# Two merge gates as seven-block products with features on the partitions, and a new layout of that phase's entry, borders and exit

## The chip, the cores and the metric

The kernel runs on one core of one Trainium2 chip. The metric is the device time of one execution in microseconds (us), the median of several runs. A profile is one execution recorded by the hardware profiler. PE is TensorE's matmul stream and PEld its weight loads, DVE is VectorE, ACT ScalarE, POOL GpSimd, and SP the engine that issues most transfers; L12 is line 12 of the kernel.

## The reference

One layer of a decoder trunk on 512 tokens of width 2048, all in float32. A normalised and modulated input `u` is projected once into the columns of three token mixers: A (differential attention), B (retention) and C (dilated windows). Each mixer's output is multiplied by a SiLU gate, projected back to width 2048, and the three are added under merge gates:

```python
u = rms_norm(x, norm_w) * (1.0 + scale[:, None]) + shift[:, None]
proj = jnp.einsum('bsd,de->bse', u, w_in)          # values, queries, keys, z, and g_a, g_b, g_c
...
y_a = jnp.einsum('bsw,wd->bsd', o_a.astype(dt) * jax.nn.silu(a_z), w_proj_a)   # y_b, y_c alike
merged = jax.nn.sigmoid(g_a) * y_a + jax.nn.sigmoid(g_b) * y_b + jax.nn.sigmoid(g_c) * y_c
y = jnp.einsum('bsd,de->bse', merged, w_out)
return x + gate[:, None] * y
```

`shift`, `scale` and `gate` (the adaLN modulation) are products of silu(c) with `w_ada`. A last RMSNorm follows.

## The kernel before, in words

**Arithmetic.** A float32 product is made of three matmuls: every operand is split into a high part that TensorE takes (`...h`, cast on ACT) and the rest (`...l`, a subtraction on DVE), and `mm3` (L144-148) adds h·h, l·h and h·l into one PSUM bank. `w_half` (L130) loads 1024 x 128 weights (`wr`, 512 KB on SP's queue) and splits them into `wh`, `wl`. `proj` (L150) multiplies 2048 x 128 weights with all 512 tokens: 2 x 8 blocks x 3 = 48 matmuls of 128x512, features on the partitions; between its halves it may call a function, `mid`. There are eight PSUM banks: two of the tag `pj` (projections), six of `at`.

**Stages.** By the trace of before, in us from the span's start: the modulation, `u` and sixteen blocks of C's merge gate (to 239); the seven-block phase (239 to 667); eight heads of C (671 to 1374); C's merge (to about 1470); heads of A (to 1765) and A's merge (to about 2045); heads of B (to 2249) and B's merge (to about 2515); the output product and the last norm.

**Seven-block phase** (L474-626). The five value matrices (2048 x 1024 each: three of C, one each of A and B) are multiplied by a scheme that splits tokens, depth and columns in two and needs seven block products where eight are usual. `unit_jobs` (L524) makes 14 jobs for one matrix of 1024 columns: P1, P2 and R3 take weights as they are (two jobs each), and eight jobs take sums of weights, one block row j each, for R6, R5, R7 and Q4. A job is 24 matmuls of 128x512; stationary are 128 tokens, moving are 512 columns. A job's preparation loads weights (`xr`, 1 MB), sums them if need be on DVE, casts `xh` on ACT and subtracts `xl` on DVE; it is issued one job ahead. The token side is fixed: four sums of token blocks, `fh` and `fl`, which `forms_build` (L496) makes from the stored `u` for two j at a time, ahead of each of the first four jobs. `keep`, `p2_done` and `sum_done` take results out of PSUM and store them to `v_dram` from GpSimd's queue (`store`).

**Entry.** The last seven raw products of C's gate are copied out of their banks by `spill` (L395), alternately on ACT and DVE, through two buffers `raw`, and stored to `graw_dram` from ACT's queue. The phase's first products, P1 of unit 0, go to `at` banks.

**Exit.** After the phase the weight pool `wp2` opens on the side where the forms lay. In the heads of C, `bias_step` (L723) works out columns of C's gate bias: four loads `bw` on SP, multiplications and sums on POOL (L641-647), and a product on TensorE (L652). It is called in heads 0, 2 and so on.

**Merges.** `gate_phase` (L656) walks over 16 blocks `db` of 128 output columns. C's ("first") loads the raw gate (`gsg`), takes the sigmoid, and stores gate times y to `part_dram`. A's ("mid") and B's ("last") compute the gate with `proj` (48 matmuls) in the block before its use, then y with 24 matmuls (`y_start`: six of the eight heads' rows; the last two after it), multiply (L700), add the part sum `gpr` (L702), which has one buffer, and store (A) or split (B) the result. In A's merge `gate_aux` also makes the adaLN gate: 32 parts, three a block, each a load `gwa` of 512 KB and two operations on DVE (L1042, L1044).

**The end of a mixer.** Head 7's last steps are put off (`left`) and run as the `mid` of the first gate projections. For A they are the turn of the softmax to keys on the partitions (transposes L943, casts L950), the values' products, and `rms_gate` (L902): a sum of squares (L896-900, L905), a root (L907), a reciprocal (L908), two multiplications, and the split of y (`yh`, L212; `yl`, L213). For B they are two heads' values and `rms_gate`s.

The order in each engine's queue is made by a scheduler from the order of the code and the buffers. SP issues its transfers in order; a transfer that waits for a buffer holds those behind it.

Of the kernel before, what the change touches and what calls it, by code (L numbers as in the profile page):

```python
# [64 lines left out]
def hybrid_kernel(ctx, tc, x, c, w_in, w_pa, w_pb, w_pc, w_out, w_ada, b_ada, norm_w, lam,  # L65
# [24 lines left out]
    graw_dram = dram.tile([KC, P, S], F32, tag="graw", name="graw")  # L90
    gate_dram = dram.tile([1, D], F32, tag="gated", name="gated")
# [313 lines left out]
    for i, (phase, k) in enumerate(steps):  # L405
# [34 lines left out]
        if k == KC - 1:  # L440
            for b in range(NF):
                spill(ps[b], b + phase * (NF + NM), b % 2 == 0)
# [53 lines left out]
    def forms_build(g):  # L496

        r = wxp.tile([P, 4, 512], F32, tag="xr", name="xr", bufs=3)
        for i in range(2):
            nc.sync.dma_start(out=r[:, 2 * i:2 * i + 2, :],  # L500
                              in_=u_dram[i * HJ + 2 * g:i * HJ + 2 * g + 2].rearrange("j p t -> p j t"))
        for jj in range(2):
            d = evp.tile([P, 4, 256], F32, tag=("z", "s")[jj], name="d")
            a11, a21 = r[:, jj, 0:256], r[:, jj, 256:512]
            a12, a22 = r[:, 2 + jj, 0:256], r[:, 2 + jj, 256:512]
            dve.tensor_sub(d[:, 0, :], a21, a22)
            dve.tensor_sub(d[:, 1, :], a11, d[:, 0, :])
            dve.tensor_sub(d[:, 3, :], a21, a11)
            dve.tensor_sub(d[:, 2, :], a12, d[:, 1, :])
            j = 2 * g + jj  # L510
            act.copy(fh[j], d)
            dve.tensor_sub(fl[j], d, fh[j].bitcast(F32))

    def stat(name, j, q):

        qs = slice(q * P, (q + 1) * P)
        if name in "0123":
            return fh[j][:, int(name), qs], fl[j][:, int(name), qs]
        k = j if name == "A11" else HJ + j
        if name == "A22":  # L520
            qs = slice(256 + q * P, 256 + (q + 1) * P)
        return uh[k][:, qs], ul[k][:, qs]

    def unit_jobs(w, c0, out):  # L524
# [10 lines left out]
        def pure_mul(key, name, t, hl):  # L535
            if t == 0:
                st[key] = [at() for _ in range(2)]
            for jj in range(4):
                j = 4 * t + jj
                for q in range(2):  # L540
                    mm3(st[key][q], *stat(name, j, q), hl[0][:, jj, :], hl[1][:, jj, :], j == 0, j == HJ - 1)
# [7 lines left out]
        def store(t, half, cc):  # L549
            nc.gpsimd.dma_start(out=out[half * 256:half * 256 + 256, cc:cc + 512].rearrange("(q p) c -> p q c", p=P),  # L550
                                in_=t)

        def p2_done():
# [3 lines left out]
            store(t, 0, 0)  # L557
# [13 lines left out]
        def sum_mul(j, hl):  # L571
# [4 lines left out]
            for key, name, s in (("R6", "1", 3), ("R5", "0", 0), ("R7", "3", 1), ("Q4", "A22", 2)):  # L576
                for q in range(2):
                    mm3(st[key][q], *stat(name, j, q), hl[0][:, s, :], hl[1][:, s, :], j == 0, j == HJ - 1)

        def sum_done():  # L580
# [8 lines left out]
            store(r3, 0, 512)  # L589
# [3 lines left out]
            store(s, 1, 512)  # L593
            for q in range(2):
                dve.tensor_sub(z[:, q, :], st["Q4"][q], z[:, q, :])
            store(z, 1, 0)

        jobs = []
        for key, name, k0, cc, done in (("P1", "A11", 0, 0, lambda: keep("P1", "p1")),
                                        ("P2", "A12", 1024, 0, p2_done),  # L600
                                        ("R3", "2", 1024, 512, lambda: keep("R3", "r3"))):
            for t in range(HJ // 4):
                jobs.append((lambda k0=k0, cc=cc, t=t: pure_prep(k0 + t * 512, c0 + cc),
                             lambda hl, key=key, name=name, t=t: pure_mul(key, name, t, hl),
                             done if t == HJ // 4 - 1 else None))
        for j in range(HJ):
            jobs.append((lambda j=j: sum_prep(j), lambda hl, j=j: sum_mul(j, hl),
                         sum_done if j == HJ - 1 else None))
        return jobs


    jobs = []
# [15 lines left out]
    wp_es, wp = open_pool("wp2", "right", reuse_waits="tile")  # L628
    y_es, yp = open_pool("yp", "right")
    g_es, gp = open_pool("gp", "right")  # L630
# [25 lines left out]
    def gate_phase(g0, w_p, mode, mh=None, ml=None, left=(), then=None, aux=None):  # L656
# [4 lines left out]
        def run_left():  # L661
            if left:
                left.pop(0)()

# [7 lines left out]
        def gate_cols(db):  # L672
# [5 lines left out]
            else:  # L678
                act.activation(out=sgs[db], in_=proj(g0 + db * P, mid=run_left), func=AF.Sigmoid)

        if mode == "first":
            for db in range(3):
                ahead[db] = y_start(db)
                run_left()
        gate_cols(0)
        for db in range(KC):
            if db + 1 < KC:
                gate_cols(db + 1)
            while left:
                run_left()  # L690
# [17 lines left out]
            if aux is not None:  # L708
                aux()


    c_es, cp = open_pool("cp", "left")
# [142 lines left out]
    for hd in range(8):  # L855
# [16 lines left out]
        if hd == 0:  # L872
# [15 lines left out]
    gate_phase(G_C, w_pc, "first", left=left)  # L888
    c_es.close()
# [112 lines left out]

    gm_es, gmp = None, None

# [251 lines left out]
```

## Time and profile before

| | |
|---|---|
| median of 3 runs | 2702.05 us (2701.15 to 2705.34) |
| the profiled execution | 2704.7 us, span 2702.9, mean granted clock 0.989 |
| TensorE busy | 2602.8 us, 96%, 11939 matmuls |
| DVE, ACT, POOL busy | 1531.2, 990.5, 231.5 us |
| moved by DMA | 405.01 MB, 150 GB/s over the span |

A row of a timeline has the start, the length, the engine and line, what is written from what, partitions x elements, a count, and in brackets the idle time ahead with what ended it. A matmul's recorded length overlaps the next one's, so the time a matmul takes from TensorE is the distance of two starts. A row of windows has, after the stretch and its length, each engine's busy us with a count in the order PE, PEld, DVE, ACT, POOL, then the granted clock (1.00 is full speed), the busy share of the DMA engines and GB/s. A row of waits has the waiting line, what it waited for, the us in total, the number of times and the longest. A row of groups has the count, then busy us and the mean ns of one, then the idle time ahead.

### The profile page before, as it was taken

The numbers are of one execution on the slowest core, as the hardware profiler recorded it, in microseconds if no ns is written. First come the engines' busy times: TensorE is split into PE (matmuls) and PEld (weight loads), VectorE is DVE, ScalarE is ACT, GpSimd is POOL, SyncE is SP. The second block draws the span as 40 slices with busy tenths as digits, with TensorE's granted clock in tenths as the row PEclk, the third lists the DMA queues.
The fourth block names the chain that finished last, engine by engine and source line by source line (L and its number), as shares of the span: only waits on it lengthen the run. The fifth ranks groups of instructions, "written<-read, shape, count | busy, mean of one in ns | idle before, by whom it ended". The sixth has DMA issues, their size and how long they took to land.

```text
span 2702.9 us, 30651 instructions
## 1 busy us (share of the span) xinstructions
PE 2602.8 (96%) x11939; PEld 2148.6 (79%) x11939; DVE 1531.2 (57%) x2283; ACT 990.5 (37%) x1399; POOL 231.5 (9%) x217
## 2 busy tenths in 40 slices
PE   7897999999999999999999999999999999999998
PEld 5675777777778888888888888888888777888888
DVE  7983877778333434444344677667336786333334
ACT  4222433333333333433333566642223454222222
POOL 3331000000231022220100000000000000000000
PEclk9998999999999999999999999999999999999999
DMA  9774666664543434434355222349544333333532
GB/s 348 246 272 159 229 210 213 217 205 166 148 113 98 133 106 110 133 98 133 102 171 164 85 79 86 94 145 307 148 143 119 86 94 96 115 114 101 206 102 102
DMA packets 467002, 405.01 MB, mean 150 GB/s; under 512 B 23509, under 2 KB 390823, under 8 KB 465703
## 3 DMA queue, kind: packets, MB, share of 16 engines
q1 hardware_dynamic: 442854, 371.49, 44.8%
q10 hardware_dynamic: 19714, 16.86, 1.8%
q0 software_dynamic: 4288, 14.72, 1.5%
q8 instruction: 93, 1.52, 0.2%
q14 instruction: 53, 0.43, 0.1%
HBM read 371.48 MB, written 31.53 MB: 149 GB/s over the span
## 4 chain that ended last, share of the span: by engine, by line
PE 78%; DVE 3%; issue 3%; DMA 2%; ACT 1%; POOL 1%; SPq 0%; DVEq 0%; POOLq 0%; ACTq 0%
PE pj L146 16%; PE pj L148 16%; PE pj L147 16%; PE at L148 9%; PE at L147 9%; PE at L146 9%; DMA bw<-in_w_in_dram 1%; DMA wr<-in_w_in_dram 1%; DVE rt L1073 1%; DVE wl L142 1%; DVE k1l L981 0%; PE at L925 0%; PE at L828 0%; PE at L781 0%; PE at L924 0%
## 5 line engine op out<-in xcount | busy, mean ns | idle before, releaser
L148 PE MATMUL pj<-uh,wl 128*128 128x512 f32 x2064 | 810.2, 393 | 13.0 <-DVE wl L142 10.5
L146 PE MATMUL pj<-uh,wh 128*128 128x512 f32 x2064 | 813.9, 394 | 3.6 <-ACT wh L141 3.6
L147 PE MATMUL pj<-ul,wh 128*128 128x512 f32 x2064 | 807.8, 391 | 0.0
L142 DVE TENSOR_TENSOR wl<-wr,wh 128x1024 fp32r<-128x1024 f32 x290 | 360.5, 1245 | 546.9 <-ACT wh L141 528.2
L141 ACT CAST wh<-wr 128x1024 fp32r<-128x1024 f32 x292 | 306.9, 1052 | 798.1 <-PE pj L147 588.3
L148 PEld LDWEIGHTS pj<-uh,wl 128*128 128x128 f32 x2064 | 390.0, 189 | 97.5 <-DVE wl L142 13.1
L146 PEld LDWEIGHTS pj<-uh,wh 128*128 128x128 f32 x2064 | 390.3, 189 | 82.9 <-ACT wh L141 4.2
L147 PEld LDWEIGHTS pj<-ul,wh 128*128 128x128 f32 x2064 | 390.4, 189 | 78.5
L146 PE MATMUL at<-yh,wh 128*128 128x512 f32 x384 | 149.7, 390 | 0.0
L148 PE MATMUL at<-yh,wl 128*128 128x512 f32 x384 | 149.6, 389 | 0.0
L147 PE MATMUL at<-yl,wh 128*128 128x512 f32 x384 | 149.5, 389 | 0.0
L567 ACT CAST xh<-xr 128x2048 fp32r<-128x2048 f32 x40 | 76.5, 1914 | 133.3 <-DVE xr L566 67.9
L146 PE MATMUL at<-xh,uh 128*128 128x512 f32 x240 | 95.5, 403 | 23.6 <-ACT xh L531 23.6
L566 DVE TENSOR_TENSOR xr<-xr 128x512 f32<-128x512 f32 x160 | 109.1, 689 | 8.8 <-DMA xr<-in_w_in_dram 5.6
L568 DVE TENSOR_TENSOR xl<-xr,xh 128x2048 fp32r<-128x2048 f32 x40 | 91.6, 2291 | 27.5 <-ACT xh L567 27.5
L700 DVE TENSOR_TENSOR gsg<-at,gsg 128x512 f32<-128x512 f32 x48 | 33.1, 690 | 117.1 <-PE at L148 93.8
L147 PE MATMUL at<-xl,uh 128*128 128x512 f32 x240 | 96.3, 401 | 2.9 <-DVE xl L532 2.9
L147 PE MATMUL at<-xl,fh 128*128 128x512 f32 x240 | 95.0, 396 | 1.4 <-DVE xl L532 1.4
L148 PE MATMUL at<-xh,ul 128*128 128x512 f32 x240 | 96.0, 400 | 0.0
L532 DVE TENSOR_TENSOR xl<-xr,xh 128x2048 fp32r<-128x2048 f32 x30 | 68.6, 2288 | 47.5 <-ACT xh L531 47.5
L148 PE MATMUL at<-xh,fl 128*128 128x512 f32 x240 | 94.8, 395 | 0.0
L146 PE MATMUL at<-xh,fh 128*128 128x512 f32 x240 | 94.0, 395 | 0.0
(365 smaller groups left out, 3835.7 us busy)
## 6 DMA issues: line engine op xcount, KB each, us to landing
wr<-in_w_in_dram SPq DMA_DIRECT2D x260, 512.0 KB, 3.9
xr<-in_w_in_dram SPq DMA_DIRECT2D x80, 512.0 KB, 4.0
xr<-in_w_in_dram SPq DMA_DIRECT2D x30, 1024.0 KB, 5.4
wa<-in_w_ada_dram SPq DMA_DIRECT2D x20, 1024.0 KB, 9.9
gwa<-in_w_ada_dram SPq DMA_DIRECT2D x32, 512.0 KB, 5.6
wr<-in_w_out_dram SPq DMA_DIRECT2D x32, 512.0 KB, 3.9
wr<-in_w_in_dram SPq DMA_DIRECT2D x32, 448.0 KB, 5.7
wb<-in_w_ada_dram SPq DMA_DIRECT2D x12, 1024.0 KB, 9.3
```

What stands on the lines that cost most here:

```text
L141: act.copy(h, r)
L142: low.tensor_sub(l, r, h.bitcast(F32))
L146: nc.tensor.matmul(ps, lhsT=ah, rhs=bh, start=start, stop=False)
L147: nc.tensor.matmul(ps, lhsT=ah, rhs=bl, start=False, stop=False)
L148: nc.tensor.matmul(ps, lhsT=al, rhs=bh, start=False, stop=stop)
L532: dve.tensor_sub(l, r, h.bitcast(F32))
L566: dve.tensor_add(r[:, o, :], r[:, o, :], r[:, a, :])
L567: act.copy(h, r)
L568: dve.tensor_sub(l, r, h.bitcast(F32))
L700: dve.tensor_mul(sg, py, sg)
L1073: dve.tensor_mul(t2[to:to + 32, :], ps[at_:at_ + 32, :], sin[at_:at_ + 32, :])
```

## The change

1. **The gates of A and B move into the seven-block phase.** Each gate (2048 columns) becomes two more units, so there are nine. They are computed feature-major (`fm`): stationary are 128 columns of weights, moving are 256 tokens, and a job is 48 matmuls of 128x256. `put_gates` takes the sigmoid and stores to `gate_of`. A's and B's merges load it and multiply y alone.
2. **Entry.** The first job's weights are prepared before the raw copies are queued, the copies go through four tiles that are two blocks wide each, and P1 goes to `pj` banks. The token sums are built for one j per job, over the first eight jobs, and the order of jobs is: P1 and P2 of unit 1, all of unit 0, then R3 and the sums of unit 1 (whose P1 goes through `p1_dram`), then the other units.
3. **Exit.** `wp2` opens on the left side and stays open to the end; the bias loads move from SP's queue to GpSimd's; the `bias_step` of head 0 moves to head 1.
4. **Merges.** All three start y for three blocks ahead, with one step of `left` after each. The adaLN gate is spread over C's merge and A's, 16 parts each, one a block (two in the first).

```diff
+    def block_mul(pss, name, j, h, l, fm):
+        if fm:
+            b = tokens(name, j, slice(0, 256))
+            for cb in range(4):
+                cs = slice(cb * P, (cb + 1) * P)
+                o = pss[cb // 2][:, (cb % 2) * 256:(cb % 2) * 256 + 256]
+                mm3(o, h[:, cs], l[:, cs], *b, j == 0 and cb % 2 == 0, j == HJ - 1 and cb % 2 == 1)
+        else:
+            for q in range(2):
+                mm3(pss[q], *tokens(name, j, slice(q * P, (q + 1) * P)), h, l, j == 0, j == HJ - 1)
...
+    def put_gates(g, b0):
+        def put(t, half, cc):
+            act.activation(out=t, in_=t, func=AF.Sigmoid)
+            b = b0 + cc // P
+            nc.gpsimd.dma_start(out=gate_of[g][b:b + 4, :, half * 256:half * 256 + 256].rearrange("b p t -> p b t"),
+                                in_=t.rearrange("p q (a t) -> p (q a) t", a=2))
+        return put
...
-    jobs = []
-    for unit, c0 in ((2, C_V), (3, C_V + 1024), (4, C_V + 2048), (0, A_V), (1, B_V)):
-        jobs += unit_jobs(w_in, c0, v_dram[unit])
+    units += [unit_jobs(w_in, g + b0 * P, put_gates(g, b0), fm=True) for g in (G_A, G_B) for b0 in (0, 8)]
+    jobs = units[1][0] + units[0][0] + units[0][1] + units[1][1]
+    for plain, summed in units[2:]:
+        jobs += plain + summed
     ready = jobs[0][0]()
+    for n, b in enumerate([NF - 1] + list(range(NF - 1))):
+        if n % 2 == 0:
+            t = evp.tile([P, 2, 512], F32, tag=("p1", "c", "r3", "s")[n // 2], name="raw")
+        (act.copy if n % 2 == 0 else dve.tensor_copy)(t[:, n % 2, :], ps[b])
+        nc.scalar.dma_start(out=graw_dram[NF + NM + b], in_=t[:, n % 2, :])
     for i, (_, mul, done) in enumerate(jobs):
-        if i < HJ // 2:
-            forms_build(i)
         nxt = jobs[i + 1][0]() if i + 1 < len(jobs) else None
+        if i < HJ:
+            form_build(i)
         mul(ready)
...
-            nc.sync.dma_start(out=r, in_=w_in[q * 512:(q + 1) * 512, G_C + db * P:G_C + (db + 1) * P]
+            nc.gpsimd.dma_start(out=r, in_=w_in[q * 512:(q + 1) * 512, G_C + db * P:G_C + (db + 1) * P]
...
-                act.activation(out=sgs[db], in_=proj(g0 + db * P, mid=run_left), func=AF.Sigmoid)
-        if mode == "first":
-            for db in range(3):
-                ahead[db] = y_start(db)
-                run_left()
+                nc.sync.dma_start(out=sgs[db], in_=gate_of[g0][db])
+        for db in range(3):
+            ahead[db] = y_start(db)
+            if left:
+                left.pop(0)()
...
+    def gate_aux(db):
+        for _ in range(2 if db == 0 else 1):
+            if gsum:
+                gate_sum()
+            if db < KC - 1:
+                gate_part()
...
-        if hd == 0:
+        if hd == 1:
             bias_step()
...
-    gate_phase(G_C, w_pc, "first", left=left)
-    c_es.close()
+    gate_phase(G_C, w_pc, "first", left=left, then=lambda: gate_open(c_es), aux=gate_aux)
+    gm_es.close()
```

What the change does to the order in ACT's queue is shown at three places. Lines of the changed kernel are a few further on: its L144 is L141 of before, its L549 L531, its L215 L212.

At the entry, ACT before: `raw` are the copies of raw gate products, `xh` the cast of a job's weights, `fh` the token sums.

```order
L398 COPY raw<-at 128x512
L401 DMA graw<-raw 128x512 x2
L398 COPY raw<-at 128x512
L401 DMA graw<-raw 128x512 x2
L398 COPY raw<-at 128x512
L401 DMA graw<-raw 128x512 x2
L398 COPY raw<-pj 128x512
L401 DMA graw<-raw 128x512
L531 CAST xh<-xr 128x2048
```

And now:

```order
L549 CAST xh<-xr 128x2048 x2
L650 COPY raw<-at 128x512 x2
L651 DMA graw<-raw 128x512
L650 COPY raw<-pj 128x512
L651 DMA graw<-raw 128x512 x5
L650 COPY raw<-at 128x512
L517 CAST fh_1820<-d 128x1024
L651 DMA graw<-raw 128x512
L549 CAST xh<-xr 128x2048
```

Two casts of weights now stand ahead of the copies, and no store stands between the first two copies.

At the exit of the phase, ACT now: `r`, `s` and `z` are results of the last gate unit, `wh` the first weights of C's head 0.

```order
L581 CAST xh<-xr 128x2048 x6
L633 ACTIVATE r_7294<-r_7294 128x1024
L633 ACTIVATE s<-s 128x1024
L633 ACTIVATE z<-z 128x1024
L144 CAST wh<-wr 128x1024 x5
```

Before, the casts of `wh` followed those of `xh` at once; three sigmoids now stand between them.

In A's tail, ACT before: `gsg` is a gate of the merge, `wh` the weights of gate projections and of y, the rest head 7's last steps.

```order
L141 CAST wh<-wr 128x1024
L896 ACTIVATE sq<-at 64x512
L896 ACTIVATE rs<-at 64x512
L899 CAST sqs<-sq 64x512
L141 CAST wh<-wr 128x1024
L679 ACTIVATE gsg<-pj 128x512
L907 ACT_TABLE_LOAD
L907 ACTIVATE rs<-at,eps 128x512
L212 CAST yh_4441<-rs 128x512
```

And now:

```order
L1034 CAST pth<-at 128x4x128
L980 ACTIVATE sq<-at 64x512
L980 ACTIVATE rs<-at 64x512
L983 CAST sqs<-sq 64x512
L991 ACT_TABLE_LOAD
L991 ACTIVATE rs<-at,eps 128x512
L215 CAST yh_7804<-rs 128x512
L144 CAST wh<-wr 128x1024 x3
```

No weights are cast and no gate is made between head 7's steps; the weights of y for the next blocks come behind its end.

More of the change, by code (lines that the diff above doesn't have):

```diff
@@ L439, in hybrid_kernel @@
             mod_step(2 if i == 0 else 1)
-        if k == KC - 1:
+        if k == KC - 1 and phase == 0:
             for b in range(NF):
-                spill(ps[b], b + phase * (NF + NM), b % 2 == 0)
+                spill(ps[b], b, b % 2 == 0)
             if phase == 0:
@@ L556, in p2_done @@
                 dve.tensor_add(t[:, q, :], st["p1"][:, q, :], st["P2"][q])
-            store(t, 0, 0)
+            put(t, 0, 0)
+            if early:
+                nc.gpsimd.dma_start(out=p1_dram, in_=st["p1"])
         def sum_prep(j):
```

196 lines of the change are left out of this document (93 added, 103 removed).

## The prediction

> **What bounds the kernel now.** I read the page first, then PE's waits, then PE's timeline at each wait.
>
> ```profile
> PE 2602.8 (96%) x11939; PEld 2148.6 (79%) x11939; DVE 1531.2 (57%) x2283; ACT 990.5 (37%) x1399; POOL 231.5 (9%) x217
> PE 78%; DVE 3%; issue 3%; DMA 2%; ACT 1%; POOL 1%; SPq 0%; DVEq 0%; POOLq 0%; ACTq 0%
> PE at L146 <- ACT xh L531: 23.6, 5, 17.5
> PE at L652 <- POOL br L647: 6.7, 1, 6.7
> PE at L781 <- DVE kc L188: 4.3, 1, 4.3
> ```
>
> TensorE is busy 96% of the span and owns 78% of the chain. Time is won by fewer or shorter matmul slots, or at the few waits; the largest, 17.5 us, stands where the seven-block phase begins. The terms below are made against the profiled execution (2704.7 us, span 2702.9); the median of the runs shown, 2702.05, lies 2.7 lower. A measurement of this kernel can tell about 0.2%, 5.4 us, from no change.
>
> **1. Gate products.** Starts of matmuls: the first of a gate's 48 and the first after them; then two 256-wide ones of the output product, 14 steps apart; then a weight load.
>
> ```profile
> 1812.30 0.39 PE L146 MATMUL pj<-uh,wh 128*128 128x512 f32 x1
> ...
> 1823.18 0.39 PE L146 MATMUL at<-yh,wh 128*128 128x512 f32 x1
> 2679.27 0.28 PE L146 MATMUL pj<-lh,mh 128*128 128x256 f32 x1
> ...
> 2680.92 0.28 PE L148 MATMUL pj<-lh,ml 128*128 128x256 f32 x1
> L148 PEld LDWEIGHTS pj<-uh,wl 128*128 128x128 f32 x2064 | 390.0, 189 | 97.5 <-DVE wl L142 13.1
> ```
>
> A 512-wide slot is 10.88/48 = 0.2267 us, a 256-wide one 1.65/14 = 0.1179. Two gates leave 2 x 16 x 48 = 1536 wide slots (348.2 us); four units bring 4 x 14 x 48 = 2688 narrow ones (316.9): **-31.3**. Bounds: 0.1200, the longest step between those rows, gives -25.6; half a wide slot, 0.1133, gives -43.6. I take the middle row, because it too changes its 128x128 weights at each matmul.
>
> The Trainium skill (TensorE: Matmul & The Clock Gate, "The mechanism") says that a weight load overlaps running matmuls only when its row group differs, and "LDWEIGHTS" there prices a load at 128/1.2 = 107 ns. By that rule a narrow slot would be 107 + 107 ns, an estimate of 0.213 us, and the phase would cost 575 us. The 0.1179 of the row disagrees: loads of 189 ns are recorded and the next start still comes after 118.
>
> **2. Entry.** TensorE's last raw product, the phase's first matmul, the second unit's and the third's first (one job of 24 into each unit); windows; ACT's last raw copy; what VectorE does from 238.8 to 300, by groups.
>
> ```profile
> 238.67 0.39 PE L434 MATMUL pj<-uh,wl 128*128 128x512 f32 x1
> 256.57 1.22 PE L146 MATMUL at<-xh,uh 128*128 128x512 f32 x2 [17.51 <-ACT xh L531]
> 351.75 0.63 PE L146 MATMUL at<-xh,uh 128*128 128x512 f32 x2
> 353.90 0.50 PE L146 MATMUL at<-xh,uh 128*128 128x512 f32 x1 [1.52 <-ACT xh L531]
> 431.93 0.64 PE L146 MATMUL at<-xh,uh 128*128 128x512 f32 x2
> 256.00:262.00 6.00, 4.33 (x9) 3.01 (x10) 4.94 (x9) 1.97 (x3) 0.00 (x0) 0.50 0.33 95
> 268.00:274.00 6.00, 5.32 (x24) 4.00 (x23) 3.72 (x5) 4.71 (x5) 0.00 (x0) 1.00 0.94 343
> 253.63 0.58 ACT L398 COPY raw<-pj 128x512 f32<-128x512 f32 x1 [7.34 <-DMA graw<-raw]
> L532 DVE TENSOR_TENSOR xl<-xr,xh 128x2048 fp32r<-128x2048 f32 x6 | 13.7, 2288 | 10.3 <-ACT xh L531 10.3
> L512 DVE TENSOR_TENSOR fl<-d,fh 128x1024 fp32r<-128x1024 f32 x8 | 9.4, 1218 | 0.5 <-ACT fh L511 0.5
> L509 DVE TENSOR_TENSOR d<-xr,d 128x256 f32<-128x256 f32 x8 | 3.3, 417 | 0.0
> ```
>
> A steady unit, border included, takes 431.93 - 351.75 = 80.2; less the border (1.7, its 1.52 of wait and the hop) 78.5, so 0.2336 per matmul and 5.6 per job. From 238.67 to 351.75 lie 113.1, for one unit and one job, 84.1: the entry loses 29.0 (the wait, half clock 0.50 behind it, and some waits on VectorE). The cause is ACT: its raw copies wait for their own stores with two buffers, up to 7.34, and the first xh cast stands behind them. Now the cast is ahead, the copies have four tiles, and P1 uses banks that the raw products leave free. What can be late next: in the first eight jobs (44.8 of TensorE) VectorE has eight xl (18.3), eight fl (9.7), 32 subtractions (13.3), and some 4 us of copies and sums, 45 to 46; the loads are 8 MB of weights, 4 of tokens and 2 to 3 of raw stores, near 45 us at the 343 GB/s row. Both are as long as the cover, so I leave 5 us: **-24** (2 to 12 left: -27 to -17).
>
> **3. Exit, and head 0 and 1 of C.** The last sums on VectorE, the first weight cast, TensorE behind it, and the clock after each of the three waits.
>
> ```profile
> 668.53 1.28 DVE L595 TENSOR_TENSOR z<-at,z 128x512 f32<-128x512 f32 x2
> 669.59 1.04 ACT L141 CAST wh<-wr 128x1024 fp32r<-128x1024 f32 x1 [11.75 <-DMA wr<-in_w_in_dram]
> 670.69 0.50 PE L146 MATMUL pj<-uh,wh 128*128 128x512 f32 x1 [3.63 <-ACT wh L141]
> 671.00:677.00 6.00, 5.52 (x19) 4.09 (x18) 2.74 (x3) 2.10 (x2) 0.00 (x0) 0.72 1.07 353
> 729.00:735.00 6.00, 6.00 (x23) 4.99 (x23) 2.68 (x7) 2.70 (x3) 0.00 (x0) 0.72 0.56 175
> 768.00:774.00 6.00, 6.00 (x16) 4.74 (x17) 0.76 (x2) 0.00 (x0) 2.23 (x3) 0.53 0.48 134
> ```
>
> Before: waits 3.6, 4.3 and 6.7 and, in 6 us each at a clock of 0.72, 0.72 and 0.53, 1.7, 1.7 and 2.8 us of lost speed: 20.8. After: the weight tiles are free early, but the order puts three sigmoids ahead of the first cast on ACT. The last can start only when the sums end, at 669.81; with one cast's 1.04 as its price it ends near 670.9, and the weight cast at 671.9. So the first wait grows by 1.3, to 4.9. POOL's bias sum is as near to its use as before, only a head later: its 6.7 and 2.8 stay. The wait on kc had its loads behind bias loads on SP's queue, which move to GpSimd's; I leave 1. (Behind the bias loads on GpSimd's queue stand only POOL's own sums and the small transfers of the head.) Sum 4.9 + 1.7 + 9.5 + 1 = 17.1: **-4** (-10, if the bias sum comes free too, to +2).
>
> **4. Borders.** Four borders of 1.7 become eight. A gate unit's hoisted matmul is half as wide; between nothing and 1.7 I take 0.9 for each of the four: **+3** (0 to +7).
>
> **5. Tails of A and B.** Gate projections covered head 7's tails; now 18 products of y, 4.1 us, stand at each place. The last score, the last softmax block, the squares, and the root of norms:
>
> ```profile
> 1759.93 0.40 PE L925 MATMUL at<-k1l,q 128*128 128x512 f32 x1
> 1773.20 0.75 DVE L934 SCALAR_TENSOR_TENSOR e<-e,st 128x512 f32<-128x512 f32 x1
> 1784.54 0.59 ACT L896 ACTIVATE sq<-at 64x512 f32<-64x512 f32 x1 [0.99 <-PE at L148]
> 1787.14 0.69 DVE L900 TENSOR_TENSOR sqs<-sq,sqs 64x512 fp32r<-64x512 f32 x1 [0.69 <-ACT sqs L899]
> 1791.57 1.28 ACT L907 ACT_TABLE_LOAD   x1
> 1793.59 3.35 DVE L908 RECIPROCAL rs<-rs 128x512 f32<-128x512 f32 x1 [1.40 <-ACT rs L907]
> 1798.49 0.62 ACT L212 CAST yh<-rs 128x512 fp32r<-128x512 f32 x1 [4.93 <-DVE rs L910]
> ```
>
> A: scores end at 1760.3; 21 projections (4.8) and 18 y reach 1769.2, the last block is ready at 1773.95; three y and ten transposes fill about 1.2: 3.5 of wait. The values' squares take 1784.54 to 1787.83, 3.3, under 18 y: no wait. From the norm's product to yh lie 7.5 with the table load (1791.57 to 1799.11), 6.2 without; six y cover 1.4: 4.8 to 6.1, taken 5.6. A: 9.1. B, from the end of its last projection: 18 y, values, 18 y, norm, values, 18 y end at 16.5. Head 6's chain (6.1 of products, 3.3 of squares, PE free at 10.2, then 7.5) gives yh at about 17.9: 1.4 of wait. One rs tile serves both heads, so head 7's squares follow yl: 1.3 more; then its 6.2, uncovered, 6.1. B: 8.8. The two last waits are longer than the 4.3 above and earn its 1.7 of slow clock each: **+21** (12 to 28).
>
> **6. Merges.** Stage rows of A's merge, and the part sum's addition and its loads (the answer on its tile):
>
> ```profile
> 1840.00:1860.00 20.00, 20.00 (x90) 16.58 (x89) 14.31 (x20) 5.23 (x6) 0.00 (x0) 1.00 0.96 303
> 1860.00:1880.00 20.00, 20.00 (x90) 16.55 (x89) 15.26 (x20) 5.42 (x7) 0.00 (x0) 1.00 0.99 332
> L702 DVE TENSOR_TENSOR gsg<-gsg,gpr x32: 672/692/693, 1801.4 to 2519.6; 128x512 f32<-128x512 f32 x32
> DMA to landing us min/median/max: 2.6/3.6/6.4
> ```
>
> A block of y is 24 x 0.2267 = 5.44 us. In A's merge it moves 512 KB of weights, 512 of the adaLN gate, 256 of gate, 256 of part sum in and 256 out: 1.835 MB, which at the mean of those rows, 317 GB/s (share 0.96 and 0.99, so no more is to be had), takes 5.79. Fifteen blocks: +5, and some at its uneven start: +9 (3; 25 if the single part-sum buffer sets the round at 6.4 + 0.7 = 7.1). C's merge moves 1.57 MB, 5.0, under 5.44: +2 (0 to 8). B's has no adaLN part: 0. **+11**. In the phase each gate unit adds four sigmoids to ACT, 1.04 each by the cast's row. What is queued behind one is the next xh cast; one job lies between that cast and its use, 5.6 us, so they are hidden while ACT keeps under it: **+1** for where two meet.
>
> **Sum:** -31.3 - 24 - 4 + 3 + 21 + 11 + 1 = -23.3: 2681.4 for such an execution, 2679 against the median.
>
> **Rivals.**
> (a) The loads of A's merge set its pace at the part sum's 7.1 us, and C's at 6.0. For: shares of 0.96 to 0.99 already with a third of the products now taken away. Against: the median landing is 3.6, a round of 4.3. It adds 16 + 6: 2701. By the Trainium skill (DMA: Bandwidth & Descriptors, "Anatomy of one DMA", for GpSimd's path) 256 KB take 2.0 + 0.6 us, an estimate of 2.6; the trace's minimum agrees, its median and maximum do not.
> (b) Slower: y's weights come one block late. SP issues in order, and a part-sum load waits for the last block's sum with the next weights behind it. If only one block lies between, a block takes the addition 0.7, a landing of 5.0 (between 3.6 and 6.4), cast 1.04, subtraction 1.2: 7.9, so 2.5 x 13 blocks in A and as much in B, +65 less the 9 of A: 2735. It decides from 6.6 us a block on. Against: the order issues weights three blocks ahead.
> (c) The entry is bound by VectorE or DMA: 20 us stay instead of 5: 2694.
> (d) A narrow slot can't hide a weight load and lasts as long as one: with the 189 ns row, 2688 x 0.189 = 508 instead of 317: 2870. It decides from 0.127 a slot. Against: the 0.1179 row. The rule of the Trainium skill in 1 would have it so.
>
> **How the numbers follow.** Forecast 0.73. The bounds of its terms, without A's 25, won't all fall one way; as the root of their squares they are 19 below and 15 above: 2660 to 2694. (a) 0.10, (b) 0.04, (c) 0.10, (d) 0.03. I give 2657 to 2700: it takes in (c) and most of (a), and leaves (b), (d) and some of the unknown beyond. Faster: forecast, (c) and a third of (a), 0.86; same 0.07; slower 0.07.
>
> **What would show it.** Right: gate units of 79 us each; no wait over 3 us between 240 and 300; two waits of about 6 us before the first finished y block of A and B; A's merge at 5.6 to 6.2 us a block with a DMA share near 1. Wrong: narrow slots over 0.125; a block of A's merge of 7 us; head 7's waits under 5 or over 15 in one tail; an entry that still loses over 15.

## The result and the profile after

The changed kernel takes 2724.68 us (median of four runs, 2722.84 to 2726.41) against 2703.07 for the kernel before (2701.15 to 2705.34): a ratio of 1.008, 95% interval 1.0062 to 1.0097. The forecast was 2679, in a range of 2657 to 2700. The change made the kernel slower where the prediction had it faster, and the time lies outside the range.

The page of the changed kernel:

```profile
span 2721.8 us, 33257 instructions
PE 2608.9 (96%) x13091; PEld 2184.7 (80%) x13091; DVE 1698.1 (62%) x2455; ACT 1034.2 (38%) x1388; POOL 265.2 (10%) x271
L151 PE MATMUL pj<-uh,wl 128*128 128x512 f32 x1552 | 616.6, 397 | 11.2 <-DVE wl L145 8.7
L149 PE MATMUL pj<-uh,wh 128*128 128x512 f32 x1552 | 620.5, 400 | 4.8 <-ACT wh L144 4.8
```

And its longest waits of TensorE (us in total, times, longest), but for those of the first stage:

```profile
PE at L149 <- ACT yh L215: 11.7, 3, 6.4
PE at L688 <- POOL br L683: 10.2, 1, 10.2
...
PE at L149 <- ACT wh L144: 6.6, 2, 6.0
```

The entry's wait of 17.5 us is gone from the list, and what came in its place is what the prediction listed: 11.7 on `yh` in the tails, a bias sum, 6.0 on a cast of weights in a merge. In sum these waits are near what the forecast has for them, so they don't explain the miss. (`yh` is the high part of a mixer's gated output, the operand of y; `kc` and `k0h`, below, are keys in the heads of C and of B.) The two group rows of the page give it away: a projection of 128x512 is recorded with 397 and 400 ns where the kernel before had 393 and 394:

```profile
L148 PE MATMUL pj<-uh,wl 128*128 128x512 f32 x2064 | 810.2, 393 | 13.0 <-DVE wl L142 10.5
L146 PE MATMUL pj<-uh,wh 128*128 128x512 f32 x2064 | 813.9, 394 | 3.6 <-ACT wh L141 3.6
```

The starts show it without overlap. First, 96 matmuls of projections in a head of C, before: the first one's start, and that of the matmul behind the last.

```profile
995.26 0.45 PE L146 MATMUL pj<-uh,wh 128*128 128x512 f32 x1
...
1017.09 0.28 PE L781 MATMUL at<-kc,qh 128*128 128x256 f32 x1
```

And the same 96 in the changed kernel:

```profile
1030.59 0.45 PE L149 MATMUL pj<-uh,wh 128*128 128x512 f32 x1
...
1053.04 0.28 PE L865 MATMUL at<-kc,qh 128*128 128x256 f32 x1
```

21.83 us have become 22.45: a slot (the distance of two neighbouring starts) takes 0.2339 where it took 0.2274, with no wait in either stretch, the same shapes and the clock at 1.00. Taken over every pair of neighbouring matmuls of one shape whose starts lie under 0.3 us apart, the mean slot of the heads' projections is 0.2333 (0.2276 before), of y 0.2334 (0.2269 before). The 512-wide slots of the output product went the other way, from 0.2324 to 0.2267.

By stage, from the starts of the first and last matmuls of each, and to the last matmul's end (the forecast's terms put to the stage they belong to):

| stage | before, us | after, us | measured | forecast |
|---|---|---|---|---|
| start and seven-block phase | 666.7 | 969.7 | +303.0 | +296.9 |
| exit and heads of C | 695.7 | 708.4 | +12.7 | -4 |
| C's merge to B's merge | 1152.6 | 858.8 | -293.8 | -316.2 |
| output product, end | 179.6 | 176.6 | -3.0 | 0 |
| sum | 2694.6 | 2713.5 | +18.9 | -23.3 |

The miss is 42 us, and 39 of it lie in the second and third rows, where the 512-wide matmuls of heads and merges are.

### The profile page after: what moved, and what is told of

It reads as the page before. It is cut to its first block, busy times and chain, and to the rows that moved or that the text cites. A ratio compares the mean times of both kernels' runs of the same rounds, so it can differ in the third digit from the quotient of the medians.

```text
span 2721.8 us, 33257 instructions
## 1 busy us (share of the span) xinstructions
PE 2608.9 (96%) x13091; PEld 2184.7 (80%) x13091; DVE 1698.1 (62%) x2455; ACT 1034.2 (38%) x1388; POOL 265.2 (10%) x271
## 4 chain that ended last, share of the span: by engine, by line
PE 77%; DVE 12%; DMA 6%; ACT 2%; issue 2%; POOL 0%; SPq 0%; ACTq 0%; DVEq 0%; POOLq 0%
PE pj L151 15%; PE pj L149 14%; PE pj L150 14%; PE at L150 10%; PE at L151 10%; PE at L149 10%; DVE acc L309 3%; DMA xr<-in_w_in_dram 2%; DVE xl L550 1%; DMA part<-gsg 1%; DVE rs L992 1%; DVE rt L1102 1%; DVE wl L145 1%; ACT xh L549 1%; DMA gpr<-part 1%
## 5 line engine op out<-in xcount | busy, mean ns | idle before, releaser
L151 PE MATMUL pj<-uh,wl 128*128 128x512 f32 x1552 | 616.6, 397 | 11.2 <-DVE wl L145 8.7
L149 PE MATMUL pj<-uh,wh 128*128 128x512 f32 x1552 | 620.5, 400 | 4.8 <-ACT wh L144 4.8
L150 PE MATMUL pj<-ul,wh 128*128 128x512 f32 x1552 | 614.8, 396 | 0.0
L144 ACT CAST wh<-wr 128x1024 fp32r<-128x1024 f32 x228 | 238.8, 1049 | 562.7 <-PE pj L150 411.3
L151 PEld LDWEIGHTS pj<-uh,wl 128*128 128x128 f32 x1552 | 293.5, 189 | 83.0 <-DVE wl L145 11.2
L149 PEld LDWEIGHTS pj<-uh,wh 128*128 128x128 f32 x1552 | 293.7, 189 | 69.8 <-ACT wh L144 5.0
L581 ACT CAST xh<-xr 128x2048 fp32r<-128x2048 f32 x72 | 137.6, 1912 | 238.6 <-PE at L150 89.1
L582 DVE TENSOR_TENSOR xl<-xr,xh 128x2048 fp32r<-128x2048 f32 x72 | 164.8, 2290 | 46.3 <-ACT xh L581 46.2
L149 PE MATMUL at<-yh,wh 128*128 128x512 f32 x384 | 156.5, 408 | 18.3 <-ACT yh L215 11.7
L550 DVE TENSOR_TENSOR xl<-xr,xh 128x2048 fp32r<-128x2048 f32 x54 | 123.7, 2291 | 54.3 <-ACT xh L549 54.1
L549 ACT CAST xh<-xr 128x2048 fp32r<-128x2048 f32 x54 | 103.0, 1910 | 128.4 <-PE at L150 51.0
L150 PE MATMUL at<-fl,xh 128*128 128x256 f32 x384 | 108.1, 281 | 0.0
L149 PE MATMUL at<-fh,xh 128*128 128x256 f32 x384 | 108.1, 281 | 0.0
L151 PE MATMUL at<-fh,xl 128*128 128x256 f32 x384 | 108.1, 281 | 0.0
```

What stands on the lines that cost most here:

```text
L144: act.copy(h, r)
L149: nc.tensor.matmul(ps, lhsT=ah, rhs=bh, start=start, stop=False)
L150: nc.tensor.matmul(ps, lhsT=ah, rhs=bl, start=False, stop=False)
L151: nc.tensor.matmul(ps, lhsT=al, rhs=bh, start=False, stop=stop)
L549: act.copy(h, r)
L550: dve.tensor_sub(l, r, h.bitcast(F32))
```

## The experiments

What distinguishes those matmuls before and after is where their weights lie. In the kernel before, the weight pool of heads and merges opened on the right side of the memory, as the token operand did; in the changed one it opens on the left. By the addresses that the built programs assign, the right side's large tiles start at 224 modulo 256 bytes (the remainder of the address divided by 256) in each partition (token operand 163808, token sums 98272, weights 139232), the left side's at 96 (weights now 31072, weights of the seven-block phase 43360). **Theory (distance):** the length of a slot depends on the distance of the moving and the stationary operand's addresses modulo 256 bytes. **Rival (side or traffic):** it depends on the side, the transfers and casts beside it, the longer program, or the new order of the queues.

**Shift the left side by 128 bytes**, in the changed kernel and in the one before:

```diff
     daw = const.tile([P, 1], F32, tag="daw", name="daw")
+    const.tile([P, 32], F32, tag="shift", name="shift")
```

> The changed kernel with one unused tile of 128 bytes per partition added to the constants, so that everything in the left pools lies 128 bytes higher; nothing else changes. Theory (distance): a 512-wide slot takes 0.2267 us when the moving and the stationary operand have the same address modulo 256 bytes, and about 0.2330 when they lie 128 apart. In the changed kernel the weights of the heads and merges went from the right side (224 modulo 256, as the token operand) to the left (96). With the shift all left tiles are at 224: some 5,800 slots of heads and merges lose 0.006 us each (35 us), 1,680 of the value units 0.0055 (9 us), the gate units little: about 2680 us, medians of slots 0.227 in heads, merges and value units. Rival (side or traffic): the slots are longer because weights on the left share something with transfers and casts, or because the code is longer; 128 bytes change nothing: 2725 within 5 us, slots stay at 0.232 to 0.233.

> The kernel before with the same unused 128 bytes in the constants. Theory (distance): the heads stay at 0.2267 (both operands right); the value units go from 0.2335 to 0.227 (1,680 slots, 11 us) and the 512-wide slots of the output product from 0.2325 to 0.2267 (768 slots, 4.5 us): about 2687 us. Rival (side or traffic): 2703 within 4 us, and slots of value units stay at 0.233.

The changed kernel takes 2694.59 with the shift; the kernel before, on that chip, 2704.92: ratio 0.9964 (0.9952 to 0.9976), where the change without it had 1.008. An unused tile of 128 bytes is worth more than the whole change cost. The same stretch of 96 matmuls:

```profile
1027.52 0.44 PE L150 MATMUL pj<-uh,wh 128*128 128x512 f32 x1
...
1049.39 0.28 PE L866 MATMUL at<-kc,qh 128*128 128x256 f32 x1
```

21.87 us, 0.2278 a slot, close to the 0.2274 of before the change. The kernel before, shifted, falls to 2692.46 (ratio 0.9952, 0.9937 to 0.9967): its heads stay at 0.2275, its value units go from 0.2333 to 0.2271, its output product from 0.2324 to 0.2266. Theory's slots all came out; the rival's did not. The times fell short: 30 us less where 45 were expected, and 12.5 where 16 were. For the changed kernel the trace shows two reasons, which make some 7 of the 15 us; the rest is open. The gate units' 256-wide slots grew, from 0.1190 to 0.1202 (3 us), and the wait at the first head of B grew by 3.5 (`k0h`, 1.0 to 4.5): there shorter slots ended in a wait for ACT.

The kernel before gains from the tile as well. With it the two kernels take nearly the same, 2692.46 and 2694.59 us, so the forecast gain of 23 us does not come back when all large operands lie at equal addresses.

**Shift the right side instead**, under the token operand, so that only some pairs change their distance; once in the changed kernel and once in the kernel before:

```diff
     u_es, up = open_pool("up", "right")
+    up.tile([P, 32], F32, tag="shift", name="shift")
```

> The changed kernel with the 128 unused bytes on the right side, below the token operand: the token operand stays at 224 modulo 256, the right pools under it (token sums of the value units, y, the first stage's weights) move from 224 to 96; the left pools stay at 96. Theory (distance): y's slots (1,152) and those of the value units that use the token sums (5 of 7 products) go to 0.227; projections of the heads stay at 0.233; the first stage's products (768), which were at 0.227, go to 0.233. Together about -7 -7 +5: 2716 us. A theory of an absolute address (left tiles must lie at 224) has no slot faster: 2725 or more. Rival (side or traffic): no slot changes, 2725.

> The kernel before with 128 unused bytes on the right side below the token operand, so that its weights lie 128 away from the tokens (96 against 224 modulo 256) in projections of the heads and of the gates; y and its weights stay at equal addresses, and the token sums of the value units come to equal ones (96). Theory (distance): 6,192 projections and 768 products of the first stage take 0.2328 instead of 0.2270 (+40 us), 1,200 slots of the value units 0.2270 instead of 0.2335 (-8): 2728 to 2735. That would be the price that the change paid, without any part of the change. Rival: 2703 within 5.

In the changed kernel, 2720.5 us (ratio 1.0055, 1.0038 to 1.0072): y goes to 0.2274 and the value units' products with token sums to 0.2273, while projections stay at 0.2333, value products with the tokens themselves at 0.2326, and the first stage's rise from 0.2275 to 0.2326. Within one run and one stage, the pairs at equal addresses are short and those 128 apart are long. An absolute address is excluded: here the left tiles lie at 96 as in the changed kernel, and their pairs with right tiles at 96 are short. The kernel before rises to 2730.73 (1.009, 1.0073 to 1.0106), inside the expected 2728 to 2735; against the 2705.82 that it takes on that chip without the tile it is 25 us more, where the theory had 25 to 32. Nothing of the change is in that kernel. Its stretch of 96:

```profile
996.64 0.45 PE L147 MATMUL pj<-uh,wh 128*128 128x512 f32 x1
...
1019.09 0.28 PE L782 MATMUL at<-kc,qh 128*128 128x256 f32 x1
```

22.45 us, the changed kernel's to the last digit.

**Undo the part of the change that moved the weights**, and nothing else:

```diff
-    wp_es, wp = open_pool("wp2", "left", reuse_waits="tile")
+    wp_es, wp = open_pool("wp2", "right", reuse_waits="tile")
...
     y_es.close()
+    wp_es.close()
     u_es.close()
+    wp_es, wp = open_pool("wp3", "right", reuse_waits="tile")
```

> The changed kernel with one part of the exit undone: the weight pool of heads and merges opens on the right side as before, and again for the output product. Theory (distance): heads and merges are back at 0.2267 (-35 us), the 512-wide slots of the output product at 0.2325 (+4.5), the value units stay at 0.233; the wait at the exit, bound by the sigmoids ahead of the first cast, stays near 4.9: about 2694 us. Rival (the slots are longer because of the queues' new order and its waits): heads stay at 0.233, 2725 within 6 us. Both agree that the waits behind A's tail (5.4 and 6.4 us) stay.

2708.92 (1.0016, 1.0006 to 1.0025), 16 us under the change, with heads at 0.2278, y at 0.2275, the output product back at 0.2324: the slots as expected, the time 15 us above. From start to start, the exit's wait fell by 1 to 4.1; the wait on `k0h` (4.0) and one more on `yh` at B's tail (3.6) ate some of the rest.

This run restores just what the forecast had left as it was, and it is still 4 us above the kernel before on that chip (2704.92), 27 from the forecast gain. In the profiled executions (2704.27 against 2704.7) 23 are left, and by the stages of the table 14 of them lie between C's merge and B's. There the matmuls themselves came out about 3 us from the forecast, but against the kernel before the waits of TensorE grew from 13.7 to 47.6, and the slow clock (half the time at a granted clock of 0.50 outside the waits, an estimate from the trace's clock) from 3.4 to 12.0: 42 us more, where the forecast has 32 for tails and merges.

**Other distances.** The same unused tile with 48 and with 16 words:

> The changed kernel with 192 unused bytes among the constants: left tiles lie at 32 modulo 256, right ones at 224. Theory A (a 512-wide slot is 0.2267 only at equal addresses modulo 256): slots of heads, merges and value units are near 0.232, as without the shift; the time near 2720. Theory B (only a distance of 128 is slow): they are 0.227, a gain of some 44 us in the 512-wide slots, 2680. For the 256-wide slots the runs so far show 0.1131 where the moving operand lies 64 below the stationary one and 0.1200 at equal addresses; the gate units' moving operand (224) now lies 64 below the stationary one (32), so by both theories their 2,688 slots go from 0.1188 to about 0.1131, 15 us: A 2710, B 2665.

> The changed kernel with 64 unused bytes among the constants: left tiles at 160, right ones at 224 modulo 256. Heads and merges have the moving operand 64 above the stationary one, the value units 64 below, the gate units 64 above. By A 512-wide slots stay near 0.232; by B 0.227. The 256-wide slots of the gate units should be 0.1175, as at that distance in the output product: 3 us less than at 128. A: 2718; B: 2678.

2720.64 (1.0069, 1.0054 to 1.0084) and 2711.2 (1.0032, 1.0017 to 1.0048). For the 512-wide slots neither theory is quite right: it isn't equality alone, and 128 isn't the only long distance. All kernels together, moving minus stationary address modulo 256, by the addresses of every matmul in the built programs, mean slot in us:

| distance | 512 wide | 256 wide |
|---|---|---|
| 0 | 0.2266 to 0.2279 | 0.1200 to 0.1203 |
| 64 | 0.2290 to 0.2297 | 0.1178 to 0.1181 |
| 128 | 0.2324 to 0.2334 | 0.1186 to 0.1191 |
| 192 | 0.2333 to 0.2338 | 0.1134 to 0.1163 |

Each row holds for all products of that width that occur at its distance (projections, y, value units, gate units, output product), whichever side they lie on; the few 256-wide products inside the heads, with means of 0.123 to 0.126, are left out. For wide slots the period of 256 shows as well: distances of 0 and 256 modulo 512 have 0.2275 and 0.2271, distances of 128 and 384 have 0.2331 and 0.2328. Wide slots are shortest at equal addresses and narrow ones longest there.

**The bias sum.** With the shift of 128, the extra bias step two projections earlier, or the bias loads back on SP's queue:

```diff
+        if hd == 1:
+            bias_step()
         ps = proj(cq + 2048, mid=lambda: scores(1, *q2, kc2))
...
-        if hd == 1:
-            bias_step()
```

> The changed kernel with the shift of 128 bytes, and the extra step of the bias in head 1 two projections earlier, so that GpSimd's four rounds (7 to 8 us each) have some 22 us more before TensorE asks for their sum. If the wait of 10.7 us on the bias sum at head 2 is that step's placement, it goes, with 2 to 3 us of slow clock behind it: 13 us less than with the shift alone, about 2682. If GpSimd is simply too slow for a column a head, the wait moves to another head and the time stays at 2694.

> The changed kernel with the shift of 128 bytes, and the bias loads back on SP's queue (undoing one part of the exit; the extra step stays late in head 1). If GpSimd's own queue makes each of the four rounds longer (0.8 us of issue and 3 to 4 of landing, against 6.0 to 7.3 a round before), the wait on the bias sum at head 2 falls from 10.7 to about 7 and the heads of C by 4 to 6 us with the slow clock behind it: about 2690. If the loads on SP hold up weights again, as the wait of 4.3 us on kc in head 0 of the kernel before, a new wait of 4 to 5 us comes in the first heads and the time stays at 2694.

The earlier step gives 2680.66 (0.9924, 0.9904 to 0.9943), as expected; the heads of C go from 691.8 us to 675.7. So in the two profiled executions the wait of 10.7 went, and 16.1 with it; the whole time fell by 13.9 in the medians and by 11 in the ratios to the kernel before on each chip (0.9964 and 0.9924). How much more than its length the wait cost is therefore not settled. Part of it is the clock. In windows of the changed kernel at the wait's end and behind it (the clock stands ahead of the DMA share) it is 0.70 over the 6 us of the second, which costs some 2 us:

```profile
1151.00:1157.00 6.00, 0.34 (x2) 0.34 (x2) 0.00 (x0) 0.00 (x0) 2.95 (x6) 0.50 0.15 44
1157.00:1163.00 6.00, 6.00 (x21) 4.80 (x21) 1.91 (x3) 0.00 (x0) 2.91 (x4) 0.70 0.47 134
1163.00:1169.00 6.00, 6.00 (x32) 4.99 (x31) 2.42 (x3) 2.02 (x3) 3.01 (x5) 1.00 0.33 92
```

With the loads on SP's queue the wait is 7.0, as the first theory has it, but a wait of 1.9 on `kc` comes in head 0 and the time is 2695.55 (0.9966, 0.9952 to 0.998), no better than with the shift alone (0.9964): both theories were half right. GpSimd's rounds in the changed kernel, from one issue to the next:

```profile
1135.19 0.76 POOL L675 DMA_DIRECT2D bw<-in_w_in_dram  x1 [0.29 <-POOL br L680]
1142.86 0.79 POOL L675 DMA_DIRECT2D bw<-in_w_in_dram  x1 [0.29 <-POOL br L683]
1150.41 0.79 POOL L675 DMA_DIRECT2D bw<-in_w_in_dram  x1 [0.30 <-POOL br L683]
```

A round lasts 7.6 us; in the kernel before, with the loads on SP's queue, the additions that end a round (753.84, 759.87, 767.10) are 6.0 and 7.2 apart.

**A's merge.** The loads of the adaLN parts (with the shift alone), or of the part sums (with the last kernel below), moved from SP's queue to GpSimd's: `nc.sync.dma_start` becomes `nc.gpsimd.dma_start` in `gate_part`, or in `gate_phase`.

> The changed kernel with the shift of 128 bytes, and the loads of the adaLN parts moved from SP's queue to GpSimd's; bytes are the same. Order theory (in A's merge the next weights stand on SP's queue behind part sums and adaLN parts that wait for buffers, which gives the wait of 5.9 us on a cast of weights and the 2.8 after it): they shrink under 3 in all, about 2688. Bandwidth theory (the stage moves all that the transfers can): the waits stay at 8 or more in all, 2694 or more.

> As the run before it, with the loads of the part sums moved from SP's queue to GpSimd's (bytes and buffers unchanged). Order theory: in A's merge the next weights no longer stand behind part sums that wait for the last block, so the wait of 5.5 us on the cast of weights goes, and the 1.6 behind it: 6 us less, about 2659. Bandwidth theory: the wait stays or moves to another load of the stage; no less than 2663.

Neither gained: 2695.42 (0.9968, 0.9957 to 0.9979) against 2694.59 (0.9964), and 2682.0 (0.9906, 0.9891 to 0.9921) against 2677.34 below. That wait on the cast of weights went away in both, as the order theory said, and others of the same size or more came. With the adaLN loads on GpSimd's queue:

```profile
2135.59 0.80 PE L760 MATMUL pj<-gh,ones_r 128*128 128x512 f32 x1 [4.22 <-ACT gh L785]
2142.16 0.80 PE L761 MATMUL pj<-gl,ones_r 128*128 128x512 f32 x1 [5.77 <-DVE gl L786]
```

These are the sums of adaLN parts, now late, and TensorE's queue stands behind them. With the part sums there, A's merge took 126.3 us instead of 113.6, from the first start of y to the last, with four waits of 1.0 to 3.2 on `wl` and two of 2.2 and 3.0 on the adaLN sums. SP's order decided where the stage waits, and no order tried made it shorter. That the transfers' rate is the limit is not shown, since their share in those stretches was 0.82 to 0.97.

**The gate units' distance.** With the shift and the earlier bias step, the gate units' weights lie 64 bytes higher inside their tiles, so that the narrow slots come to distance 192 and the wide ones keep 0:

```diff
+        o = 16 if fm else 0
...
-                wxp.tile([P, 4, 512], F32R, tag="xh", name="xh", bufs=2),
+                wxp.tile([P, 2112], F32R, tag="xh", name="xh", bufs=2)[:, o:o + 2048].rearrange("p (a c) -> p a c", a=4),
```

> The kernel with the shift of 128 bytes and the earlier bias step; besides, the four gate units lay their weights 64 bytes higher inside their tiles, so that the moving tokens (224 modulo 256) lie 64 below the stationary weights (32). By the distances measured so far a 256-wide slot goes from 0.1200 to 0.114, 2,688 x 0.006 = 16 us: 2665 instead of 2681. If at that distance another limit of the phase comes up (VectorE's or the transfers' pace of a job at 5.6 us), the gain is half or less: 2673 or more.

2677.34 us (ratio 0.9893, 0.9878 to 0.9908), the fastest of all, but not 16 us under the run with the bias step: 3 by the medians, 8 by the ratios (0.9924 there, on another chip), whose intervals overlap. The narrow slots are 0.1163 on the mean, in two groups at 0.113 to 0.114 and 0.117 to 0.118. Starts in one stretch of each kind, 12 steps apart, and then of the run with the part sums on GpSimd's queue:

```profile
699.77 0.28 PE L152 MATMUL at<-fh,xl 128*128 128x256 f32 x1
...
701.18 0.28 PE L152 MATMUL at<-fh,xl 128*128 128x256 f32 x1
744.62 0.28 PE L152 MATMUL at<-fh,xl 128*128 128x256 f32 x1
...
745.98 0.28 PE L152 MATMUL at<-fh,xl 128*128 128x256 f32 x1
699.82 0.28 PE L150 MATMUL pj<-fh,xh 128*128 128x256 f32 x1
...
701.18 0.28 PE L150 MATMUL at<-fh,xh 128*128 128x256 f32 x1
```

These are 0.1175, 0.1133 and 0.1133 a slot. The two buffers of `xh` lie at distances of 192 and 448 modulo 512, but that doesn't part the groups: the mean with `xh` is 0.1157 at the one and 0.1161 at the other, and the run with the part sums on GpSimd's queue has the same addresses and 0.1137 and 0.1140. One stretch of jobs keeps one length and the next has the other, so at 192 a narrow slot has two lengths, and what chooses between them is open.

Of the 2,688 x 0.0040 = 10.8 us that the mean slot gives, the phase kept 4.7 (725.4 to 720.7): the waits on `xl` in the gate units, 0.2 to 0.8 each before, are now 0.7 to 1.8, 3.7 more in sum. That is the other limit that the expectation named, but which half of it is not settled. Ahead of the longest of these waits VectorE, which makes `xl`, had itself stood for a load of weights:

```profile
752.79 0.69 DVE L582 TENSOR_TENSOR xr<-xr 128x512 f32<-128x512 f32 x1 [2.15 <-DMA xr<-in_w_in_dram]
```

## Why the prediction was wrong

**The step that failed** is a step that the sum takes without naming it: that the slots left in heads and merges stay as they were. "A block of y is 24 x 0.2267 = 5.44 us" was written of the changed kernel from a row of the one before, and of the exit only that "the weight tiles are free early". Opening the weight pool on the left moved 5,760 wide matmuls (4,608 projections, 1,152 of y) from distance 0 to distance 128. 4,608 x 0.0057 + 1,152 x 0.0065 = 34 us, less 3 in the output product, whose operands came to lie equal: 31 of the 42 us by this count. The shift of 128 bytes undoes the slots, and the kernel before with the shift on its right side reproduces them. Undone, they gave back less than they add up to: 22 us in the profiled heads and merges with the shift and 21 with the pool on the right, since part of the time then passed in waits. The clue stood in the prediction's own numbers: 0.2336 for a matmul of the value units and 0.2267 for one of the gates, both 128x512 at full clock without waits. Two lengths for one shape were taken as properties of two stages, and nothing was asked about what sets them.

**A second step was mis-sized**: the waits of tails and merges. The sum has 32 us for them (21 and 11, slow clock included). The changed kernel has 36, and with the weights on the right, where the slots are as the sum assumed, 42: the wait on `k0h`, which the sum does not have, grew by 3.8, and the slow clock by 8.6 where the sum has 3.4. So the forecast would have missed by 27 us even with the slots that it assumed.

The other steps, in the order of the prediction:

1. Gate products: right but for the slot, 0.1190 instead of 0.1179, so 3 us of -31.3 were missed. The row of the output product has distance 64, the gate units 128. The Trainium skill's rule (TensorE: Matmul & The Clock Gate, "The mechanism"), read as the prediction has it, that a load of the same row group waits for the matmul ahead and a narrow slot would be 0.213, is contradicted by all runs here (0.1134 to 0.1203), and so is rival (d). That section of the Trainium skill also lets a load go ahead into a background weight buffer; no run here shows whether that is what happens.
2. Entry: right. The phase starts 0.2 us after the last raw product (238.10 and 238.32).

```profile
238.10 0.39 PE L437 MATMUL pj<-uh,wl 128*128 128x512 f32 x1
238.32 0.40 PE L149 MATMUL pj<-xh,uh 128*128 128x512 f32 x1
408.79 0.63 PE L149 MATMUL pj<-xh,uh 128*128 128x512 f32 x2
410.95 0.50 PE L149 MATMUL at<-xh,uh 128*128 128x512 f32 x1 [1.52 <-ACT xh L549]
```

   From there to the first matmul of the third unit lie 170.5 us, for two units and one job: 696 slots of 0.2326, 161.9. So 8.6 are left where 5 were forecast, inside the bounds of 2 to 12.
3. Exit: the first wait is 4.8, forecast 4.9, and the wait on `kc` went to nothing, forecast 1. The bias sum was mis-sized: forecast 6.7 and 2.8 of slow clock, measured 10.2 and some 2 (with the shift 10.7, and 11 to 16 in all by the run that takes it away). The move to GpSimd's queue, which the prediction counted as a gain for SP alone, lengthened each of POOL's rounds.
4. Borders: value borders as before, 1.9 from start to start, but three of them, since the first two units run into each other; those of the gate units 0.9 to 1.0, where the slot's own 0.12 is part of it. Right in size. Not in the sum is a wait on `xl` in the middle of each gate unit, 0.8, 1.9, 0.8 and 0.8 from start to start.
5. Tails: right in place and size. In A 2.1, 2.1 and 5.4 from start to start (forecast 3.5 and 5.6), in B 0.7, 1.4 and 6.9 (forecast 1.4, 1.3 and 6.1).

```profile
2121.26 0.79 PE L149 MATMUL at<-yh,wh 128*128 128x512 f32 x1 [5.00 <-ACT yh L215]
2148.88 0.80 PE L149 MATMUL at<-yh,wh 128*128 128x512 f32 x1 [5.95 <-ACT wh L144]
2452.98 0.50 PE L989 MATMUL at<-sqs,ones_r 128*128 128x512 f32 x1 [1.05 <-DVE sqs L984]
2459.88 0.79 PE L149 MATMUL at<-yh,wh 128*128 128x512 f32 x1 [6.39 <-ACT yh L215]
```

6. Merges: A's has one wait of 6.0 and two of 0.8 and 1.9 (forecast 9 for the stage), right in size. The first one's cause is the mechanism of rival (b), once: SP's rows show the weights issued at 2143.11, behind three part sums, 17 us after the casts had freed the tile. It happens behind the tail, not in each block, so it cost 6 and not 65. SP's row, and then three windows of the stage that follows: in two of them the share of the transfers reaches the forecast's ceiling, between them it does not:

```profile
2143.11 0.43 SPq L130 DMA_DIRECT2D wr<-in_w_proj_a_dram  x1
```

```profile
2146.00:2166.00 20.00, 16.31 (x61) 12.73 (x62) 12.62 (x18) 4.21 (x5) 0.00 (x0) 0.83 1.00 321
2166.00:2186.00 20.00, 17.94 (x69) 13.69 (x69) 11.11 (x14) 2.69 (x3) 0.00 (x0) 0.91 0.79 251
2186.00:2206.00 20.00, 20.00 (x88) 16.21 (x87) 14.05 (x19) 6.22 (x9) 0.00 (x0) 1.00 0.99 318
```

So most of the mechanisms that the prediction weighed came out near their sizes; what it held constant did not hold. With the operands at equal addresses the changed kernel has 0.9964 and, with the bias step moved, 0.9924, but the kernel before has 0.9952 with the same tile. In the changed kernel's own trace, some 30 of the 42 us are the wide slots, 6 the start and the seven-block phase (the narrow slots 3, the entry 4, the waits inside gate units 4, less what one border fewer and shorter value slots saved), 4 the waits and slow clock from C's merge to B's, and 2 those of the exit and the heads of C.

## What to carry to other kernels

When an edit moves a pool, compare the addresses that operands of the same matmul get before and after, not only when the tiles come free; a pad of some bytes is then a cheap experiment, and the kernel before needs the same pad before the two are compared. When one shape has two lengths in a trace without a wait between, find out why before either of them is used for a forecast. And a step that makes TensorE faster lays bare waits that its slowness had hidden: restored slots gave back 21 us in heads and merges where they add up to 34.

## What the runs showed of the hardware

A 128x512 fp32r matmul with a new 128x128 stationary operand takes 0.227 to 0.234 us from start to start, depending on the distance of the two operands' addresses modulo 256 bytes: 0.2266 to 0.2279 at 0, 0.2290 to 0.2297 at 64, 0.2324 to 0.2334 at 128, 0.2333 to 0.2338 at 192. A 128x256 one takes 0.120 at 0 and at 192 either 0.113 or 0.118, for stretches of jobs, with the same addresses. Why is not shown; that it is the distance, and not the side, the absolute address or the traffic, is shown by the shifts of either side in both kernels. Behind the wait of 10.2 us on the bias sum the granted clock stayed at 0.50 for some 4 us (0.70 on the mean of the first whole window).
